# Moving the two halves of the normalised activations to other addresses, 256 and 128 bytes off the weights modulo 512

## The chip, the cores and the metric

The kernel runs on one core of one Trainium2 chip. The metric is the device time of one execution in microseconds, taken as the median of three runs.

## The reference, cut to what matters

A decoder trunk of two layers, 256 tokens wide 1024. Layer 0 mixes tokens with a dilated sliding window (three head groups of eight heads), layer 1 with block-sparse attention, which at 256 tokens is plain causal attention over one block (16 heads). Each layer ends in a squared-ReLU MLP of width 4096.

```python
for i in range(DEPTH):                       # 2
    u = rmsnorm(h, norm_mix[i])
    h = h + (dsw_mixer if i % 2 == 0 else moba_mixer)(u, w_qkv, q_gain, k_gain, w_o, rel_bias)
    h = h + sq_relu_mlp(rmsnorm(h, norm_ffn[i]), ffn_w1[i], ffn_w2[i])

def sq_relu_mlp(h, w1, w2):
    return jnp.square(jax.nn.relu(h @ w1)) @ w2
```

All inputs and outputs are float32.

## The kernel before, in words

Every large product is computed in split precision. A weight slice of 128 rows by 512 columns comes from HBM into a `raw` buffer; ScalarE writes its rounded part `hi` and VectorE the rest `lo` (`next_hi`, line 158, and `next_lo`, line 173). The activations are split in the same way. A product is then three TensorE matmuls: high by high, high by low, low by high. `mm3` (line 230) issues them for the attention projections and for the second MLP product; `up` (line 629) writes them out for the first (lines 654 to 656).

`u` is the transposed activation, before its row norm is applied (the norm's factor is multiplied in later). It stands in four SBUF tiles: `uh` and `ul` (high and low part) of half 0 (rows 0 to 511 of the model width) and of half 1. `norm_transpose` (line 347) makes them: four TensorE transposes of `h` into PSUM, a copy on ScalarE (line 362), a subtraction on VectorE (line 363). Each tile is 128 partitions by 4 chunks of 256 float32, that is 4096 bytes in a partition. `ux(k, cols)` (line 404) gives chunk `k`, from half `k // 4`.

`u` is used in two places, in opposite roles:

- `project` (line 411), the q, k and v projections of both layers (tiles `acc_a`, `acc_b`). The chunk of `u` for one half of the tokens (128 columns, 512 bytes in a partition) is the stationary operand, loaded by LDWEIGHTS; the weight slice of 512 columns is the moving one. For each of 15 groups of columns and each half of the tokens, `k` runs from 0 to 7: twelve matmuls on half 0 of `u`, then twelve on half 1.
- `ffn`'s `up(j)`, `j` from 0 to 7 (tile `up`). Here 128 columns of a weight slice (512 bytes) are stationary and a chunk of `u` (256 columns, 1024 bytes) moves. For `j` of 1 and more, `c` runs over four column blocks and `k` from 0 to 7 inside it, so again twelve matmuls on half 0 and twelve on half 1 take turns. For `j` of 0 all of half 0 comes first.

The other large products, `down(j)` of the MLP (tile `y`) and `wo_group` (tiles `wo_a`, `wo_b`), don't use `u`: a hidden or attention tile (`hh`, `hl`, `oh`, `ol`) is stationary, and a weight slice moves. An MLP runs `up(0)`, `up(1)`, `down(0)`, `up(2)`, `down(1)` and so on to `down(7)`.

The order of work is written out by hand; weight splitting and small work are placed between the matmuls by `beat` and `defer`.

Addresses follow from the order in which pools and tiles are declared, and from their sizes, each rounded up to 32 bytes. The tiles that hold weights (`raw`, `hi`, `lo`), hidden values and attention outputs all start at a multiple of 512 bytes in the partition. Ahead of the four tiles of `u` lie `spread` (1028 bytes, from a multiple of 512) and `warm`, of which one element is used:

```python
    warm = const.tile([P, 33], F32, name="warm")                    # line 275
    ...
        if t == 0:                                                  # line 349
            u[half] = tuple(ut.tile([P, 4, S], F32R, tag=f"u{half}{s}", bufs=1, name=f"u{s}_{which}_{half}")
                            for s in ("h", "l"))
```

1028 bytes take 1056, which is 32 modulo 512; `warm` with 132 bytes takes 160; so all four tiles of `u`, each 4096 bytes long, start 192 bytes past a multiple of 512.

Of the kernel before, what the change touches and what calls it, by code (L numbers as in the profile page):

```python
# [24 lines left out]
F32 = mybir.dt.float32  # L25
F32R = mybir.dt.float32r
# [4 lines left out]
P = 128  # L31
S = 256
# [35 lines left out]
def trunk(ctx, tc, x, rel_bias, norm_mix, norm_ffn, a_w_qkv, a_q_gain, a_k_gain, a_w_o,  # L68
# [6 lines left out]
    const = ctx.enter_context(tc.tile_pool(name="const", bufs=1))  # L75

    ut = ctx.enter_context(tc.tile_pool(name="ut", bufs=1))
# [5 lines left out]
    def bank(tag, name):  # L83
        return ps.tile([P, 512], F32, tag=tag, bufs=2, name=name)
# [151 lines left out]
    h = const.tile([P, NT, D], F32, name="h")  # L236
# [35 lines left out]
                            pattern=[[-1, S + 1]], channel_multiplier=2)  # L272
    mhalf = lead.tile([P, 16], F32, name="mhalf")
    nc.gpsimd.memset(mhalf, -0.5)
    warm = const.tile([P, 33], F32, name="warm")
    nc.scalar.activation(warm[:, 0:1], ident[:, 0:1], AF.Exp)

    gt = lead.tile([P, 36], F32, name="gt")
# [65 lines left out]
    u = {}  # L344
    rstd = {}

    def norm_transpose(which, half, t, natural):

        if t == 0:
            u[half] = tuple(ut.tile([P, 4, S], F32R, tag=f"u{half}{s}", bufs=1, name=f"u{s}_{which}_{half}")  # L350
                            for s in ("h", "l"))
        tp = bank("tp", f"ut_{which}_{half}_{t}")
        for c in range(4):
            k = 4 * half + c
            nc.tensor.transpose(out=tp[:, c * P:(c + 1) * P], in_=h[:, t, k * P:(k + 1) * P], identity=ident)  # L355
        hi, lo = u[half]
        i = tp.rearrange("p (c q) -> p c q", c=4)
        if natural:
            hi, lo = (z.rearrange("p c (q t) -> p t c q", t=NT)[:, t] for z in (hi, lo))
        else:  # L360
            hi, lo = (z[:, :, t * P:(t + 1) * P] for z in (hi, lo))
        nc.scalar.activation(hi, i, AF.Copy)
        nc.vector.tensor_sub(lo, i, hi.bitcast(F32))
# [33 lines left out]
    def norm_half(which, half, natural=False, lead=2):  # L397
        for t in range(NT):
            defer(lead + t, lambda t=t: norm_transpose(which, half, t, natural))
        defer(lead + 3, lambda: norm_squares(which, half))  # L400
        if half == 1:
            defer(lead + 7, lambda: norm_scale(which, natural))
# [287 lines left out]
    for t in range(NT):  # L690
        norm_transpose(0, 0, t, False)
        keep_warm(1)
        for _ in range(2):
            next_hi()
            next_lo()
    for t in range(NT):
        defer(4 + t, lambda t=t: norm_transpose(0, 1, t, False))
# [96 lines left out]
```

## Time and profile before

| | us |
|---|---|
| median of 3 runs | 630.51 (630.36 to 631.11) |
| the profiled execution, device time | 630.4 |
| the profiled execution, span of its instructions | 628.6 |
| TensorE busy | 623.0 (99%) |
| TensorE weight loads busy | 541.2 (86%) |
| VectorE busy | 426.8 (68%) |
| ScalarE busy | 385.1 (61%) |
| DMA engines, mean rate | 181 GB/s |

The span runs from the first to the last instruction; the device time is 1.8 us longer. TensorE's clock was granted in full throughout. Matmuls overlap in their pipeline, so the busy time of TensorE is not a measure of its rate: the rate is read from the distance between the starts of matmuls that follow each other, and the duration that a row gives for one matmul grows with that distance.

### The profile page before, as it was taken

How to read it: one execution, taken by the hardware profiler on the slowest of the kernel's cores; microseconds unless marked ns; L12 is line 12 of the kernel's file. 1: busy time of each engine (PE TensorE's matmuls, PEld its weight loads, DVE VectorE, ACT ScalarE, POOL GpSimd, SP SyncE). 2: the span in 40 equal slices, each digit the busy share in tenths (PEclk: the TensorE clock that was granted, in tenths of full speed). 3: DMA queues.
4: the chain of work that ended last, by engine and by line, in shares of the span. 5: the costliest groups of instructions: out<-in, count | busy, mean ns of one | idle time of the engine just before them, and what ended most of it. 6: DMA issues, size and time to landing. Idle time of an engine off the chain costs nothing.

```text
span 628.6 us, 10380 instructions
## 1 busy us (share of the span) xinstructions
PE 623.0 (99%) x3902; PEld 541.2 (86%) x3902; DVE 426.8 (68%) x767; ACT 385.1 (61%) x742; POOL 36.6 (6%) x23
## 2 busy tenths in 40 slices
PE   8999999999999999999999999999999999999997
PEld 7778887888989989998988878778998899899886
DVE  5877988856875476467547789887776745754651
ACT  6866876765765356456537868777665644663540
POOL 1222221000000000000000332000000000000000
PEclk9999999999999999999999999999999999999999
DMA  7977456433655563574556657563467446645801
GB/s 250 315 196 241 124 187 174 163 108 124 215 174 190 205 223 140 187 254 140 174 179 202 196 180 195 142 186 125 157 211 260 147 161 230 220 127 191 250 18 68
DMA packets 74539, 113.62 MB, mean 181 GB/s; under 512 B 4585, under 2 KB 30505, under 8 KB 74489
## 3 DMA queue, kind: packets, MB, share of 16 engines
q1 hardware_dynamic: 74312, 112.82, 55.7%
q8 instruction: 31, 0.51, 0.3%
q14 instruction: 20, 0.16, 0.1%
q10 hardware_dynamic: 176, 0.14, 0.1%
HBM read 111.81 MB, written 1.13 MB: 180 GB/s over the span
## 4 chain that ended last, share of the span: by engine, by line
PE 97%; DVE 1%; DMA 1%; ACT 0%; issue 0%; DVEq 0%; SPq 0%; ACTq 0%
PE up L654 10%; PE up L656 9%; PE up L655 9%; PE y L231 9%; PE y L233 9%; PE y L232 9%; PE acc_a L231 6%; PE acc_a L232 5%; PE acc_a L233 5%; PE acc_b L231 3%; PE acc_b L233 3%; PE acc_b L232 3%; PE s_a L520 1%; PE o_a L585 1%; PE ut L355 1%; PE wo_b L231 1%
## 5 line engine op out<-in xcount | busy, mean ns | idle before, releaser
L179 DVE SCALAR_TENSOR_TENSOR lo<-raw,gt,hi 128x512 fp32r<-128x512 f32 x248 | 174.6, 745 | 7.4 <-ACT hi L169 7.2
L169 ACT ACTIVATE hi<-raw,gt 128x512 fp32r<-128x512 f32 x248 | 163.0, 714 | 5.7 <-PE y L233 2.8
L654 PE MATMUL up<-uh,hi 128*128 128x256 f32 x512 | 143.6, 281 | 0.0
L655 PE MATMUL up<-ul,hi 128*128 128x256 f32 x512 | 143.3, 280 | 0.0
L656 PE MATMUL up<-uh,lo 128*128 128x256 f32 x512 | 143.3, 280 | 0.0
L177 DVE TENSOR_TENSOR lo<-raw,hi 128x512 fp32r<-128x512 f32 x152 | 98.0, 685 | 42.0 <-ACT hi L167 41.8
L167 ACT ACTIVATE hi<-raw 128x512 fp32r<-128x512 f32 x152 | 88.1, 624 | 52.6 <-PE up L655 20.2
L231 PE MATMUL y<-hi,hh 128*128 128x512 f32 x256 | 99.8, 390 | 0.0
L233 PE MATMUL y<-hi,hl 128*128 128x512 f32 x256 | 99.6, 389 | 0.0
L232 PE MATMUL y<-lo,hh 128*128 128x512 f32 x256 | 99.6, 389 | 0.0
L656 PEld LDWEIGHTS up<-uh,lo 128*128 128x128 f32 x512 | 97.8, 191 | 0.0
L655 PEld LDWEIGHTS up<-ul,hi 128*128 128x128 f32 x512 | 96.1, 188 | 0.6
L654 PEld LDWEIGHTS up<-uh,hi 128*128 128x128 f32 x512 | 96.1, 188 | 0.5
L640 DVE TENSOR_TENSOR r<-r 128x512 f32<-128x512 f32 (+1 forms) x36 | 22.7, 631 | 65.6 <-ACT r L638 65.6
L638 ACT ACTIVATE r<-up 128x512 f32<-128x512 f32 (+1 forms) x36 | 19.8, 550 | 72.8 <-PE up L656 72.4
L231 PE MATMUL acc_a<-hi,uh 128*128 128x512 f32 x144 | 60.6, 421 | 0.0
L232 PE MATMUL acc_a<-lo,uh 128*128 128x512 f32 x144 | 57.0, 396 | 0.0
L233 PE MATMUL acc_a<-hi,ul 128*128 128x512 f32 x144 | 56.9, 395 | 0.0
L233 PEld LDWEIGHTS y<-hi,hl 128*128 128x128 f32 x256 | 48.0, 188 | 10.0
L231 PEld LDWEIGHTS y<-hi,hh 128*128 128x128 f32 x256 | 48.1, 188 | 9.4
L232 PEld LDWEIGHTS y<-lo,hh 128*128 128x128 f32 x256 | 48.1, 188 | 9.4
L231 PE MATMUL acc_b<-hi,uh 128*128 128x512 f32 x96 | 40.1, 418 | 0.0
(128 smaller groups left out, 777.4 us busy)
## 6 DMA issues: line engine op xcount, KB each, us to landing
raw<-in_ffn_w_dram SPq DMA_DIRECT2D x128, 512.0 KB, 4.9
raw<-in_a_w_qkv_dram SPq DMA_DIRECT2D x64, 256.0 KB, 4.3
raw<-in_b_w_qkv_dram SPq DMA_DIRECT2D x24, 512.0 KB, 4.6
raw<-in_b_w_o_dram SPq DMA_DIRECT2D x8, 512.0 KB, 5.0
bias_a<-vdram_a SPq DMA_DIRECT2D x20, 128.0 KB, 6.0
raw<-in_a_w_qkv_dram SPq DMA_DIRECT2D x4, 512.0 KB, 6.6
raw<-in_a_w_o_dram SPq DMA_DIRECT2D x4, 512.0 KB
bias_b<-vdram_b SPq DMA_DIRECT2D x8, 256.0 KB, 4.5
```

Source lines behind the costliest of these rows:

```text
L167: nc.scalar.activation(hi, w, AF.Copy)
L169: nc.scalar.activation(hi, w, AF.Copy, scale=gt[:, gain + c:gain + c + 1])
L177: nc.vector.tensor_sub(lo, w, hi.bitcast(F32))
L179: nc.vector.scalar_tensor_tensor(lo, w, gt[:, gain + c:gain + c + 1], hi.bitcast(F32), op0=ALU.mult, op1=ALU.subtract)
L231: nc.tensor.matmul(acc, lhsT=a[0], rhs=b[0], start=first, stop=False)
L232: nc.tensor.matmul(acc, lhsT=a[0], rhs=b[1], start=False, stop=False)
L233: nc.tensor.matmul(acc, lhsT=a[1], rhs=b[0], start=False, stop=last)
L638: defer(1, lambda: nc.scalar.activation(r, banks[b][:, :w], AF.Relu))
L640: defer(3, lambda: nc.vector.tensor_mul(r, r, r))
L654: nc.tensor.matmul(o, lhsT=whi[:, cols], rhs=uh, start=k == 0, stop=False)
L655: nc.tensor.matmul(o, lhsT=whi[:, cols], rhs=ul, start=False, stop=False)
L656: nc.tensor.matmul(o, lhsT=wlo[:, cols], rhs=uh, start=False, stop=k == 7)
```

## The change

`warm` grows from 33 to 49 elements. It takes 224 bytes in place of 160, so that the first tile of `u` starts at 256 modulo 512. The low part of half 0 gets 96 more float32, 384 bytes that nothing reads or writes, behind its data; so the tiles of half 1 start at 256 + 384, which is 128 modulo 512. The tiles keep their shape for all who use them.

```diff
-    warm = const.tile([P, 33], F32, name="warm")
+    warm = const.tile([P, 49], F32, name="warm")
@@
         if t == 0:
-            u[half] = tuple(ut.tile([P, 4, S], F32R, tag=f"u{half}{s}", bufs=1, name=f"u{s}_{which}_{half}")
-                            for s in ("h", "l"))
+            n = {"h": 4 * S, "l": 4 * S + (96 if half == 0 else 0)}
+            u[half] = tuple(ut.tile([P, n[s]], F32R, tag=f"u{half}{s}", bufs=1, name=f"u{s}_{which}_{half}")
+                            [:, 0:4 * S].rearrange("p (c q) -> p c q", c=4) for s in "hl")
```

No instruction is added, removed or moved.

## Rows read from the trace of the kernel before

**Rows 1.** The page: span, TensorE's busy time, clock, and the chain that ended last
```profile
span 628.6 us, 10380 instructions
PE 623.0 (99%) x3902; PEld 541.2 (86%) x3902; DVE 426.8 (68%) x767; ACT 385.1 (61%) x742; POOL 36.6 (6%) x23
PEclk9999999999999999999999999999999999999999
PE 97%; DVE 1%; DMA 1%; ACT 0%; issue 0%; DVEq 0%; SPq 0%; ACTq 0%
```
**Rows 2.** Waits of TensorE: waiting line, awaited one, us in total, times, longest
```profile
PE warm_ps L261 <- DVE idle L255: 1.1, 1, 1.1
PE ut L355 <- DMA h<-in_x_dram: 0.6, 1, 0.6
```
**Rows 3.** The page's costliest groups: line, shapes, count, busy us, mean ns of one
```profile
L654 PE MATMUL up<-uh,hi 128*128 128x256 f32 x512 | 143.6, 281 | 0.0
L231 PE MATMUL acc_a<-hi,uh 128*128 128x512 f32 x144 | 60.6, 421 | 0.0
L231 PE MATMUL acc_b<-hi,uh 128*128 128x512 f32 x96 | 40.1, 418 | 0.0
```
**Rows 4.** Timeline of TensorE, start and duration in us: `up(0)`, `up(1)`, then `down(0)`
```profile
156.88 0.60 PE L355 MATMUL ut<-ident,h 128*128 128x128 f32 x4
...
157.68 0.28 PE L654 MATMUL up<-uh,hi 128*128 128x256 f32 x1
...
176.03 0.28 PE L654 MATMUL up<-uh,hi 128*128 128x256 f32 x1
...
176.38 0.39 PE L231 MATMUL y<-hi,hh 128*128 128x512 f32 x1
...
177.07 0.39 PE L231 MATMUL y<-hi,hh 128*128 128x512 f32 x1
```
**Rows 5.** Timeline of TensorE: `up(2)` from its first matmul, then `down(1)`, then `up(3)`
```profile
187.27 0.28 PE L654 MATMUL up<-uh,hi 128*128 128x256 f32 x1
...
198.58 0.39 PE L231 MATMUL y<-hi,hh 128*128 128x512 f32 x1
...
209.46 0.28 PE L654 MATMUL up<-uh,hi 128*128 128x256 f32 x1
```
**Rows 6.** Groups of instructions from 158 to 176 us (`up(0)`, `up(1)`)
```profile
L655 PE MATMUL up<-ul,hi 128*128 128x256 f32 x54 | 14.9, 276 | 0.0
L654 PE MATMUL up<-uh,hi 128*128 128x256 f32 x53 | 14.6, 276 | 0.0
```
**Rows 7.** Groups of instructions from 187.3 to 331 us (`up(2)` to `down(7)`, layer 0)
```profile
L655 PE MATMUL up<-ul,hi 128*128 128x256 f32 x192 | 54.0, 281 | 0.0
L232 PE MATMUL y<-lo,hh 128*128 128x512 f32 x110 | 42.8, 389 | 0.0
```
**Rows 8.** Groups of instructions from 479.5 to 615 us (the same in layer 1)
```profile
L654 PE MATMUL up<-uh,hi 128*128 128x256 f32 x192 | 54.0, 281 | 0.0
```
**Rows 9.** Timeline of TensorE: `project` of layer 1, a stretch that nothing else interrupts
```profile
341.10 0.39 PE L232 MATMUL acc_b<-lo,uh 128*128 128x512 f32 x1
...
352.77 0.39 PE L232 MATMUL acc_b<-lo,uh 128*128 128x512 f32 x1
```
**Rows 10.** Timeline of TensorE: output projection of layer 1, such a stretch
```profile
435.71 0.50 PE L231 MATMUL wo_b<-hi,oh_b 128*128 128x512 f32 x1
436.04 0.40 PE L232 MATMUL wo_b<-lo,oh_b 128*128 128x512 f32 x1
436.28 0.39 PE L233 MATMUL wo_b<-hi,ol_b 128*128 128x512 f32 x1
...
437.20 0.39 PE L231 MATMUL wo_b<-hi,oh_b 128*128 128x512 f32 x1
...
442.41 0.39 PE L233 MATMUL wo_b<-hi,ol_b 128*128 128x512 f32 x1
```
**Rows 11.** Instructions on tile `uh`: count, ns min/median/max, first and last start
```profile
L656 PEld LDWEIGHTS up<-uh,lo x512: 187/192/192, 153.8 to 602.6; 128*128 128x128 f32 x171
L362 ACT ACTIVATE uh<-ut x16: 576/598/643, 5.3 to 450.8; 128x512 fp32r<-128x512 f32 x16
L363 DVE TENSOR_TENSOR ul<-ut,uh x16: 680/692/693, 5.9 to 451.5; 128x512 fp32r<-128x512 f32 x16
```

## The prediction, made before the changed kernel was run

> **What bounds the kernel now.** I read the page first. TensorE is busy for 623.0 of 628.6 us at full clock, and 97% of the chain that ended last is its own [rows 1]. The waits of TensorE name two, 1.1 and 0.6 us, both in the first microseconds [rows 2]. No other engine holds it up. So the time can only change with the distance from one matmul to the next, and the question is which matmuls stand further apart than they must.
>
> The page can't tell, since it averages: 281 ns for a matmul of `up`, 418 to 421 for the first of each triple of `acc` [rows 3], the latter with the gaps behind transposes in it. So I went to the timeline and divided the distance of two starts by the matmuls between them.
>
> - `up(0)` and `up(1)`: 157.68 to 176.03 us holds 162 matmuls, 113.3 ns each [rows 4].
> - `up(2)`: 187.27 to 198.58 us holds 96, 117.8 ns each [rows 5]. Same shape, same lines, same addresses modulo 512.
> - `down(1)`, the same stretch further: 198.58 to 209.46 us, 48 matmuls of 512 columns, 226.7 ns each [rows 5], just twice 113.3.
> - `project`, undisturbed: 341.10 to 352.77 us, 51 matmuls, 228.8 ns [rows 9].
> - `wo_b`, undisturbed: 437.20 to 442.41 us, 23 matmuls, 226.5 ns [rows 10].
>
> The groups of instructions by stretch confirm that these are not chosen spots: a matmul of `up` lasts 276 ns from 158 to 176 us [rows 6] and 281 ns in all of `up(2)` to `up(7)`, in both layers [rows 7, 8]. Twelve of the sixteen `up` stages therefore run at the wide pace (117.8 ns) and four at the narrow one (113.3).
>
> Two things are to be seen here. First, with stationary and moving operand both at 0 modulo 512 (`y`, `wo`) the matmuls settle at 226.7 ns; with the stationary one at 192 (`acc`) they stay 2.1 ns above it for as long as the stretch lasts. So the offset plausibly matters. Second, `up` shows both 113.3 and 117.8 ns at one and the same offset. So the offset alone doesn't decide; how a stage is entered does, and it then persists: 162 matmuls narrow, 96 wide, none in between. The wide pace follows a `down`, the narrow one follows transposes. The excess is regular, 13.3 ns in three matmuls of `up` (3 x 4.45) and about 6.5 in three of `acc` (3 x 2.15), one about twice the other, which looks like a step of some 6.7 ns lost once or twice in three matmuls (an estimate of mine, worked out from these distances).
>
> **The change part by part.** It moves no instruction. What it changes is three relations.
>
> *`up`, wide stages.* 12 stages x 96 = 1152 matmuls x (117.8 - 113.3) = 5.1 us [rows 4, 5, 7, 8]. This is the most that `up` can give. The moving `u` goes from 192 off the weights to 256 in the first twelve matmuls of each column block, and to 128 in the second twelve. No row shows either offset. The bounds of what they cost per matmul: from below, 0 over the narrow pace; from above, the nearest thing is a pace with three steps in three matmuls in place of two, that is 6.7 ns over the narrow one, 2.2 more than now. Over 1152 matmuls that is -5.1 to +2.6 us.
>
> *`up`, narrow stages.* 4 stages x 96 = 384 matmuls. They have nothing to win. If they fall to the wide pace they lose 384 x 4.45 = 1.7 us.
>
> *`acc`.* 15 groups x 2 x 8 x 3 = 720 matmuls, at most 720 x 2.15 = 1.5 us to win against the 226.7 of `y` [rows 5, 9]. To lose: as much again, if one step in three becomes two, 1.5 us.
>
> *The border between the halves.* New is that within one stage the relation jumps every twelve matmuls. Before, both halves lay alike and nothing jumped. No row shows such a jump; the nearest are two changes of operands. Where a narrow `up` meets `down(0)`, three matmuls from 176.38 to 177.07 us take 0.69 us against 0.68 when settled, 10 ns lost [rows 4]. Behind other work, `wo_b` needs 240 ns for one matmul and 230 each for four (436.28 to 437.20) where 226.5 is settled, 27 ns lost [rows 10]. I take 10 ns, since operands follow each other there without a pause, as at the border. There are 7 jumps in each of 14 `up` stages and 1 in each of 2, 100 in all, and in `project` 4 for each group but a layer's first, 54 in all: 154 jumps, 0 to 1.5 us at 10 ns, 4.2 us at 27. Below nothing it can go as well, because a jump that meets the wide pace can end it; that is counted with the stages.
>
> *What else moves.* The slack behind `ul` of half 0 is neither written nor read. The writers of `u` are 16 copies of 598 ns and 16 subtractions of 692 ns in the whole program [rows 11]; were each 10% slower, it would be 32 x 0.065 = 2.1 us of work on engines that are busy 61 and 68% of the span, and TensorE waits for neither in any row [rows 1, 2]. Without that cover it would be the 2.1 us. The small tiles behind `u` shift too; they hold a few numbers per partition. I put all this at nothing.
>
> *Which value I take.* For `up` in its wide stages, one of the two halves at the narrow pace and the other as now: 576 x 4.45 = 2.6 us won. The reason is the persistence: the wide pace lasts because each of 96 matmuls finds the same relation, the narrow pace lasts for the same reason, and of the two offsets now met in turn I take it that one is entered so that the narrow pace is reached. Each return into it costs a jump, 10 ns, four times in each of 12 stages: 0.5 us lost. For `acc` and the narrow stages, no change. Sum: 2.6 - 0.5 = 2.1 us won against the profiled execution's 630.4 us (628.6 of span and 1.8 around it, which stays), so 628.3; the median of the runs shown stands 0.1 above that execution, so 628.4.
>
> *A rule against this.* In `acc` and `y` the same moving operand (a weight slice at 0) stands further apart when the loaded one lies at 192: 228.8 against 226.7 ns [rows 5, 9]. The Trainium skill, TensorE: Matmul & The Clock Gate, section "Step-by-step: what each phase is for", says that TensorE has two independent read ports on SBUF and that loading the next weights takes no read bandwidth from the running matmul. By that rule no offset matters and the change is worth 0; the rows of `acc` and `y` speak against it, though not finally, since the two stages also differ in what runs beside them.
>
> **The rivals.**
>
> *No change: the pace is set by history, not by address.* For it: `up` shows both rates at one offset [rows 4, 5], so a stage might keep its rate wherever `u` lies; and 256 and 128 lie evenly on both sides of 192, so what one half wins the other may lose. Against it: `acc` never reaches the 226.7 ns that `y` and `wo` reach within some matmuls [rows 9, 10]. Result 630.5, from 629.3 to 631.7. That the change doesn't do what it says, because the tiles land elsewhere, ends here too; the sizes and the rounding to 32 bytes leave little room for it.
>
> *Slower: the jumps break the narrow stages.* The narrow pace needs an undisturbed run; a jump every twelve matmuls throws `up(0)` and `up(1)` of both layers to the wide pace (1.7 us), and each jump costs some matmuls of settling (0 to 1.5 us, at the far bound 4.2), while the wide stages stay as they are, because both offsets hold the same conflict. Result 630.5 + 1.7 + 0 to 1.5 = 632.2 to 633.7, at the far bound 636.4. It decides from the point where the first matmuls behind a jump stand over 113.3 ns apart in `up(0)`, whose single jump is easy to find. For it: 10 ns were lost where operands change at the narrow pace [rows 4]. Against it: `up(0)` is cut by transposes at 156.88 us and is at the narrow pace again from 157.68 at the latest [rows 4], so a disturbance need not end in the wide one.
>
> *Much faster: all of `up` narrow, and `acc` at the rate of `y`.* 5.1 + 1.5 = 6.6 us: 623.9. For it: nothing but that both rates exist. Against it: it needs both offsets, in both roles, to be free of loss.
>
> **How the numbers follow.** A measurement of this kernel can tell about 0.2%, 1.3 us, from no change. Forecast, part of the loss in `up` is gone: 0.32, from 626.0 to 629.2, most likely 628.4. Much faster: 0.10, 623.9 to 626. No change: 0.28. Slower: 0.30, of which the ends beyond 633 hold a third. The range leaves out the far end of "much faster" and the far end of "slower", about 0.1 each: 625.0 to 633.0. The forecast's own range is 626.0 to 629.2, since cases of both signs hold much. Faster by over 0.2%: 0.42; within: 0.28; slower: 0.30.
>
> **What would show it.** Right: in a wide stage such as the one that began at 187.27 us, the distance alternates every twelve matmuls between about 113.3 and 117.8 ns, and the durations of `up` by stretch show 276 beside 281; `y` and `wo` stay at 389 ns; `acc` stays near 228.8. The stage's 96 matmuls then take about 11.1 us in place of 11.31. Also to be read: LDWEIGHTS of the low weights, 192 ns at the median now against 187 at the least [rows 11], which should fall in the narrow half. Wrong: `up` at 117.8 throughout (no change), `up(0)` and `up(1)` at 281 ns (slower), or a change in `y`, which doesn't use `u` at all and would mean that the reason is another. A share of VectorE's or ScalarE's waits in the chain would mean that something I put at nothing isn't.

## The result, and the profile after

The changed kernel is slower: 635.64 us in the median of 4 runs (634.71 to 635.72) against 630.78 us (630.36 to 631.11, 4 runs) of the kernel before on the same chip, a ratio of 1.0076 with a 95% interval from 1.0064 to 1.0088. The profiled execution took 635.72 us, of which 633.9 us are span; the 1.8 us around it stayed. So 5.3 us more of span are to be found in this pair of profiles.

The page of the changed kernel answers [rows 1]: span, TensorE, its clock by slices, the chain that ended last.

```profile
span 633.9 us, 10380 instructions
PE 627.2 (99%) x3902; PEld 544.5 (86%) x3902; DVE 427.4 (67%) x767; ACT 385.8 (61%) x742; POOL 36.6 (6%) x23
PEclk8999999999999999999999999999999999999999
PE 96%; DVE 1%; DMA 1%; ACT 1%; issue 0%; SPq 0%; DVEq 0%; ACTq 0%
```

Nothing has taken the bound away from TensorE: still 99% busy, still nearly the whole chain. One digit differs, the first of the clock. The rest must again be in the distance from matmul to matmul.

Groups of instructions, first of 158 to 176 us (`up(0)`, `up(1)`; lines are one higher than before), to be held against [rows 6]:

```profile
L656 PE MATMUL up<-ul,hi 128*128 128x256 f32 x50 | 14.1, 282 | 0.0
```

and of 187.3 to 331 us (`up(2)` to `down(7)` of layer 0), to be held against [rows 7]:

```profile
L655 PE MATMUL up<-uh,hi 128*128 128x256 f32 x192 | 54.1, 282 | 0.0
...
L232 PE MATMUL y<-lo,hh 128*128 128x512 f32 x111 | 43.2, 390 | 0.0
```

`up` was at 276 and 281 ns; now it is at 282 ns in both kinds of stage. The narrow stages are gone, and the wide ones have become a little wider. The timeline of TensorE gives the pace (start, duration; the stretches of [rows 4] and [rows 5]):

```profile
159.05 0.28 PE L656 MATMUL up<-ul,hi 128*128 128x256 f32 x1
...
177.98 0.28 PE L656 MATMUL up<-ul,hi 128*128 128x256 f32 x1
...
189.48 0.28 PE L655 MATMUL up<-uh,hi 128*128 128x256 f32 x1
...
190.92 0.28 PE L655 MATMUL up<-uh,hi 128*128 128x256 f32 x1
...
192.34 0.28 PE L655 MATMUL up<-uh,hi 128*128 128x256 f32 x1
...
200.90 0.40 PE L231 MATMUL y<-hi,hh 128*128 128x512 f32 x1
...
211.82 0.28 PE L655 MATMUL up<-uh,hi 128*128 128x256 f32 x1
```

- `up(0)` and `up(1)`: 159 matmuls from 159.05 to 177.98 us, 119.1 ns each, where it was 113.3.
- `up(2)`: 96 matmuls from 189.48 to 200.90 us, 119.0 ns each, where it was 117.8. Its first twelve, on half 0, take 1.44 us, the twelve on half 1 behind them 1.42 us. Two decimals are too few for a pace over twelve: by the starts in ns these are 119.3 and 119.0 ns each, and over the 14 stages with seven jumps both halves average 119.0. Neither half is anywhere near 113.3.
- `down(1)`: 48 matmuls from 200.90 to 211.82 us, 227.5 ns, where it was 226.7.

`project` of layer 1, the stretch of [rows 9], twelve matmuls on half 0 of `u` and then twelve on half 1:

```profile
348.15 0.39 PE L231 MATMUL acc_b<-hi,uh 128*128 128x512 f32 x1
...
350.88 0.40 PE L231 MATMUL acc_b<-hi,uh 128*128 128x512 f32 x1
...
353.68 0.40 PE L231 MATMUL acc_b<-hi,uh 128*128 128x512 f32 x1
```

Half 0 takes 227.5 ns for each, half 1 about 233; before, both stood at 228.8.

Adding up all distances from one start to the next by stage, in both traces, gives the account (us, sums of my own from the starts):

| stage | before | after | difference | of which |
|---|---|---|---|---|
| `up` | 179.71 | 183.08 | +3.37 | four stages that were narrow, 2.0 together; twelve that were wide, about 1152 x 1.2 ns = 1.4 |
| `acc_a`, `acc_b` | 174.82 | 176.20 | +1.38 | half 1, about 360 x 2.2 ns = 0.8; half 0, nothing behind the start; the rest, 0.6, is the first 13 us |
| `y` | 174.11 | 174.56 | +0.45 | the first six matmuls of each `down` |
| all else | | | +0.1 | |

That is the 5.3 us. Two entries need a word. In `y` each of the 14 `down`s that follow an `up` now begins with distances of 235, 231, 236, 228, 233 and 231 ns before it settles at 226.7, since it is entered out of `up` in another step than before: 34 ns, 14 times.

The other is the start. Timeline of the changed kernel:

```profile
9.20 0.63 PE L233 MATMUL acc_a<-hi,ul 128*128 128x512 f32 x1
9.63 0.63 PE L231 MATMUL acc_a<-hi,uh 128*128 128x512 f32 x1
...
12.13 0.39 PE L231 MATMUL acc_a<-hi,uh 128*128 128x512 f32 x1
```

and of the kernel before:

```profile
9.08 0.63 PE L233 MATMUL acc_a<-hi,ul 128*128 128x512 f32 x1
9.51 0.63 PE L231 MATMUL acc_a<-hi,uh 128*128 128x512 f32 x1
...
10.64 0.40 PE L231 MATMUL acc_a<-hi,uh 128*128 128x512 f32 x1
```

In both, matmuls of 512 columns stand 0.43 us apart at first and 0.23 us later; the change comes at about 10.4 us before and at about 12.1 us in the changed kernel. A stretch of one microsecond in the changed kernel (columns: stretch and its length, TensorE's busy time and instructions, granted clock as a fraction of the 2.4 GHz level, DMA share, GB/s) shows it at 1.2 GHz:

```profile
11.00:12.00 1.00, 1.00 (x4) 0.50 1.08 381
```

The page of the kernel before shows full clock from the first slice on [rows 1], and so the text in front of the prediction says "throughout". But its trace holds no record of the clock ahead of 10.43 us, and the page counts time without a record as full; its matmuls stood 0.43 us apart there, just as those of the changed kernel did at a recorded 0.50.

The waits of TensorE in the changed kernel, against [rows 2]:

```profile
PE ut L356 <- DMA h<-in_x_dram: 0.9, 1, 0.9
PE acc_a L231 <- ACT hi L169: 0.5, 1, 0.5
PE acc_a L232 <- DVE lo L179: 0.3, 1, 0.3
```

They come to 1.1 us more than before, but that isn't time lost: behind them the third matmul of `acc_a` starts only 0.12 us later than before (9.20 and 9.08 us). They stand ahead of the fall of the clock, which in this trace was granted in full from 5.2 us and at half from 8.6 to 12.05 us. In all, the first transposes of the second half of `u` come at 12.83 us in place of 12.03. This 0.8 us is no work of the change: run e9 below, whose stages all keep the old pace, starts later still (13.23 us), e5, with other offsets again, earlier (11.85 us), and 13 runs of the kernel before on one chip lie between 630.20 and 632.13 us. So of the 5.3 us about 4.5 are the change's.

### The profile page after: what moved, and what is told of

It is laid out like the page before. It is cut to its first block, busy times and chain, and to the rows that moved or that the text cites. A ratio compares the mean times of both kernels' runs of the same rounds, so it can differ in the third digit from the quotient of the medians.

```text
span 633.9 us, 10380 instructions
## 1 busy us (share of the span) xinstructions
PE 627.2 (99%) x3902; PEld 544.5 (86%) x3902; DVE 427.4 (67%) x767; ACT 385.8 (61%) x742; POOL 36.6 (6%) x23
## 4 chain that ended last, share of the span: by engine, by line
PE 96%; DVE 1%; DMA 1%; ACT 1%; issue 0%; SPq 0%; DVEq 0%; ACTq 0%
PE up L655 10%; PE up L657 10%; PE up L656 10%; PE y L233 9%; PE y L232 9%; PE y L231 9%; PE acc_a L231 6%; PE acc_a L232 5%; PE acc_a L233 5%; PE acc_b L231 3%; PE acc_b L233 3%; PE acc_b L232 3%; PE s_a L521 1%; PE o_a L586 1%; PE wo_b L231 1%; PE pt_a L564 1%
```

## The experiments

At the start these theories stood against each other. A: each offset of `u` has a settled pace of its own in each of its two roles, and the jumps between the halves matter little. A1: the offset has one price for both roles, so that what is good in `acc` is good in `up`. B: the offsets are harmless, the jumps every twelve matmuls do the damage. C: at one offset two paces can hold, and the way in chooses. D: other work beside TensorE makes the difference, or the size and place of other tiles.

### One half's offset for both, and the halves exchanged

e1 has both halves at 256, e2 both at 128; neither has a jump.

```diff
-    warm = const.tile([P, 33], F32, name="warm")
+    warm = const.tile([P, 49], F32, name="warm")      # e1: 49, e2: 17; u as in the kernel before
```

> All four tiles of u at 256 modulo 512, no jump between the halves. Theory A (each offset has its own settled pace, the jumps cost little): matmuls of up settle at 120.0 ns, as they do at the end of each twelve on half 0 in the changed kernel, in all sixteen stages, that is 2.2 x 1152 + 6.7 x 384 ns = 5.1 us more than before; acc settles at 226.7 ns, as it does there on half 0, up to 1.2 us less; 634 to 635 us. Theory B (the loss comes from the jumps between the halves, either offset alone is no worse than 192): up at 117.8 ns or less after each down and 113.3 ns in the first two stages, 630.5 us or less.

> All four tiles of u at 128 modulo 512, no jump. Theory A: up settles near 118.8 ns, the mean of the repeating five distances 120, 119, 115, 118, 122 that half 1 shows in the changed kernel, in all stages: 1.0 x 1152 + 5.5 x 384 ns = 3.3 us more than before; acc near 231 to 232 ns, some 1.5 us more; about 635 us. Theory B: 630.5 us or less, as for 256.

e1: 634.93 us (634.72 to 635.58), ratio 1.007, 1.0055 to 1.0085. e2: 638.43 us (636.63 to 638.48), ratio 1.0115, 1.0095 to 1.0135. `up(2)` with the first matmul behind it, and 36 matmuls of `project` of layer 1, in the timeline of e1:

```profile
188.76 0.28 PE L655 MATMUL up<-uh,hi 128*128 128x256 f32 x1
...
200.27 0.40 PE L231 MATMUL y<-hi,hh 128*128 128x512 f32 x1
...
347.84 0.39 PE L231 MATMUL acc_b<-hi,uh 128*128 128x512 f32 x1
...
356.00 0.39 PE L231 MATMUL acc_b<-hi,uh 128*128 128x512 f32 x1
```

and of e2:

```profile
190.65 0.28 PE L655 MATMUL up<-uh,hi 128*128 128x256 f32 x1
...
202.17 0.39 PE L231 MATMUL y<-hi,hh 128*128 128x512 f32 x1
...
350.04 0.40 PE L231 MATMUL acc_b<-hi,uh 128*128 128x512 f32 x1
...
358.41 0.40 PE L231 MATMUL acc_b<-hi,uh 128*128 128x512 f32 x1
```

In e1 `up` stands at 119.9 ns (11.51 us over 96) and `acc` at 226.7 (8.16 us over 36); in e2 at 120.0 and 232.5. So without a single jump the loss is all there: B falls. The offset that is best for `acc`, 256, is the worst for `up`: A1 falls as well. The jumps even help a little: with them `up` takes 183.08 us, without them 184.51 (256) or 184.12 (128). On half 0 the first eight or so matmuls behind a jump are not yet settled at 120.0; on half 1 the distances repeat 120, 119, 115, 118 and 122 ns, a mean of 118.7, which is the pace of e2's `up(0)` and `up(1)` and not the 120.0 of its other stages.

e3 puts half 0 at 128 and half 1 at 256, by 17 elements of `warm` and 32 float32 of slack.

```diff
-    warm = const.tile([P, 49], F32, name="warm")
+    warm = const.tile([P, 17], F32, name="warm")
@@
-            n = {"h": 4 * S, "l": 4 * S + (96 if half == 0 else 0)}
+            n = {"h": 4 * S, "l": 4 * S + (32 if half == 0 else 0)}
```

> The halves of the changed kernel exchanged: half 0 at 128, half 1 at 256 modulo 512. Theory A: the same two paces change places (up 120.0 ns at the end of each twelve on half 1, the five distances on half 0; acc 226.7 ns on half 1), total within 1 us of the changed kernel, 634.6 to 636.6 us. Theory B: the same number of jumps and so the same loss, 635.6 us; but if a single direction of the jump does the harm, another time.

634.95 us (634.66 to 636.71), ratio 1.0075, 1.0057 to 1.0092. The paces go with the offset, not with the half: now the last matmuls on half 1 stand at 120.0 ns in `up` and settle at 226.7 in `acc`, and half 0 shows 232.5 in `acc`.

### Same offsets, other places

e4 leaves both halves at 192 modulo 512, but moves half 1 by 512 bytes, with the same kind of slack that the change brought in. e9 moves half 1 by 256 bytes, to 448.

```diff
-    warm = const.tile([P, 49], F32, name="warm")
+    warm = const.tile([P, 33], F32, name="warm")
@@
-            n = {"h": 4 * S, "l": 4 * S + (96 if half == 0 else 0)}
+            n = {"h": 4 * S, "l": 4 * S + (128 if half == 0 else 0)}      # e4: 128, e9: 64
```

> Half 0 at 192 as before, half 1 also at 192 modulo 512 but 512 bytes further up than before, so that the tiles are cut and spaced as in the changed kernel without a change modulo 512. Theories A and B alike: nothing changes, 630.5 us, up 113.3 ns in the first two stages and 117.8 ns after each down, acc 228.9 ns. A theory by which the spacing of the tiles, the padded tile or the shift of the small tiles does the harm: 632 to 636 us.

> Half 0 at 192, half 1 at 448 modulo 512, so that the relation jumps by 256 at each border of the halves. If the pattern repeats every 256 bytes, as the kernels at 0 and 256, 64 and 320, 128 and 384 suggest: nothing changes against before, 113.3 ns in the first two stages of up, 117.8 ns after each down, acc 228.9 ns, 630.2 us. If it repeats every 512, another pace on half 1 and other totals.

e4: 630.23 us (630.07 to 632.10, 10 runs), ratio 0.9995, 0.9984 to 1.0006. `up(2)` of e4:

```profile
187.02 0.28 PE L655 MATMUL up<-uh,hi 128*128 128x256 f32 x1
...
198.32 0.39 PE L231 MATMUL y<-hi,hh 128*128 128x512 f32 x1
```

11.30 us over 96 matmuls, before 11.31, and every stage's sum is that of before within 0.05 us, apart from the first 13 us. So slack, moved tiles and shifted small tiles cost nothing, and that half of D falls; the other half, work beside TensorE, falls with e11 and e14 below. e9: 631.7 us in one run beside 630.59; `up`, `y` and `acc_b` take 179.71, 174.11 and 69.40 us, as before to the hundredth, and the 1.2 us more lie in the first 13 us. An offset of 448 is thus the same as one of 192.

### A row of offsets

One run each, both halves alike, by the size of `warm`: 113 elements for 0, 1 for 64, 65 for 320, 81 for 384, 41 for 224.

```diff
-    warm = const.tile([P, 33], F32, name="warm")
+    warm = const.tile([P, 113], F32, name="warm")     # e5: 113, e6: 1, e7: 65, e8: 81, e10: 41
```

> All four tiles of u at 0 modulo 512, as the weights. Theory A1 (what counts is the offset of the loaded operand from the moving one, in any stage): acc has then the offset of y and must settle at 226.7 ns as y does; up has the offset 0 too and should settle at 113.3 ns everywhere: 630.8 less 5.1 and up to 1.6 us, about 624 us. Theory A2 (each role has its own dependence on the offset, since in up weight loads follow each other without a pause): acc 226.7 ns all the same, up anywhere between 113.3 and 120.0 ns, 624 to 634 us.

> All four tiles at 64 modulo 512. A1 and A2: acc between 226.7 (0, 256) and 233 ns (128); up between 113.3 and 120 ns; a point of the curve, 624 to 639 us. If the offsets are of no matter for up after a down, 117.8 ns.

> All four tiles at 320 modulo 512: u then stands to the weights in up as the weights stood to u in acc at 192. A1: up settles at the pace that acc has at 192, one lost step in three matmuls, 115.6 ns, and acc at the one that up has at 192 after a down, two lost steps in three, 231.1 ns: 630.8 - 2.5 + 1.0 + 1.6 = about 631 us. A2: no such exchange.

> All four tiles at 384 modulo 512, the mirror of 128. A1: up as acc at 128, that is 2.5 to 3 lost steps in three matmuls, about 119 to 120 ns; acc as up at 128, 231 to 233 ns: 636 to 639 us. A2: no such exchange.

> All four tiles at 224 modulo 512, between 192 (up 113.3 or 117.8, acc 228.9 ns) and 256 (up 120.0, acc 226.7 ns). If only the 64-byte block counts, as 192: 630.2 us. If the place inside the block counts as well, paces between or outside those, 627 to 636 us.

Paces in ns, once settled, by stage, and the sums of `up` and `acc_b` in us, from the starts of each trace (`acc_b` rather than `acc_a`, since the start of the span lies in `acc_a`):

| offset of both halves | run | time, us | `up(0)`, `up(1)` | `up(2)` to `up(7)` | `acc` | sum of `up` | sum of `acc_b` |
|---|---|---|---|---|---|---|---|
| 0 | e5 | 634.77 | 120.0 | 120.0 | 226.7 | 184.50 | 69.14 |
| 256 | e1 | 634.93 | 120.0 | 120.0 | 226.7 | 184.51 | 69.14 |
| 64 | e6 | 635.32 | 117.8 | 117.8 | 233.3 | 181.28 | 70.37 |
| 320 | e7 | 635.53 | 117.8 | 117.8 | 233.3 | 181.28 | 70.37 |
| 128 | e2 | 638.43 | 118.7 | 120.0 | 232.5 | 184.12 | 70.07 |
| 384 | e8 | 636.56 | 118.6 | 120.0 | 232.5 | 184.12 | 70.06 |
| 192 | before | 630.78 | 113.3 | 117.8 | 228.9 | 179.71 | 69.40 |
| 224 | e10 | 636.37 | 118.3 | 118.3 | 233.3 | 182.08 | 70.15 |

In both sums, pairs that differ by 256 bytes agree to 0.01 us (their times differ by up to 1.9 us, most of it in the start of `acc_a`). A1 had 624 us for e5 and 631 for e7, and missed both. What counts is the offset modulo 256, not modulo 512 as the change's own words have it; its two offsets are 0 and 128 in that measure. The weights lay at 0 modulo 512 in every run, so whether the place of `u` counts by itself or its distance from the weights is not separated. Inside the 256 bytes nothing tried comes near 192, and 224 shows that 32 bytes off it are enough to lose. Two of the traces, e6 (`up(2)` at 117.8 ns, `acc` at 233.3):

```profile
189.85 0.28 PE L655 MATMUL up<-uh,hi 128*128 128x256 f32 x1
...
201.16 0.40 PE L231 MATMUL y<-hi,hh 128*128 128x512 f32 x1
...
348.00 0.40 PE L231 MATMUL acc_b<-hi,uh 128*128 128x512 f32 x1
...
356.40 0.40 PE L231 MATMUL acc_b<-hi,uh 128*128 128x512 f32 x1
```

and e10 (`up(2)` at 118.3 ns):

```profile
190.48 0.28 PE L655 MATMUL up<-uh,hi 128*128 128x256 f32 x1
...
201.84 0.40 PE L231 MATMUL y<-hi,hh 128*128 128x512 f32 x1
```

At 64 the wide pace stands in all sixteen `up` stages, `up(0)` and `up(1)` too. The narrow pace occurs at 192 (and 448, e9) alone. So A holds as far as the offset and the role decide which paces there are, but not as one pace for each: 192 has 113.3 and 117.8, and 128 and 384 have two as well, 118.6 to 118.7 and 120.0, again by what comes ahead of the stage. What is left is C.

### The way in

The kernel before has a case of C that the prediction passed over. In layer 1 `up(0)` is entered straight from `wo_b`; its first 18 matmuls, up to the transposes that cut it, stand at the wide pace, and behind the transposes the same stage, at the same addresses, settles at the narrow one (timeline of before; 17 distances in 2.00 us, then 21 in 2.38):

```profile
446.95 0.28 PE L654 MATMUL up<-uh,hi 128*128 128x256 f32 x1
...
448.95 0.28 PE L656 MATMUL up<-uh,lo 128*128 128x256 f32 x1
...
451.36 0.28 PE L654 MATMUL up<-uh,hi 128*128 128x256 f32 x1
...
453.74 0.28 PE L654 MATMUL up<-uh,hi 128*128 128x256 f32 x1
```

e11 and e12 leave `u` at 192 and send one more matmul ahead of the first of each `up(j)` from `j` = 2 on, over 258 or 268 columns; the first matmul proper starts its bank anew and so overwrites it. e14 is the same with 256 columns, a shift by no more than a whole matmul.

```diff
                     cols = slice(c * P, (c + 1) * P)
+                    if j >= 2 and c == 0 and k == 0:
+                        nc.tensor.matmul(banks[b][:, 0:258], lhsT=whi[:, cols],      # e12: 268, e14: 256
+                                         rhs=u[0][0].rearrange("p c q -> p (c q)")[:, 0:258], start=True, stop=True)
                     nc.tensor.matmul(o, lhsT=whi[:, cols], rhs=uh, start=k == 0, stop=False)
```

> The kernel before with one matmul more at the head of each up after a down (12 in all): the first one is issued twice, the first time over 258 columns in place of 256, its result overwritten; so the 96 that follow start some 0.8 ns later than they would behind 256. Theory C (at 192 both paces are stable, and the entry picks one): if the shift reaches the narrow pace, 96 matmuls at 113.3 ns in those stages, 12 x (96 x 4.45 - 133) ns = 3.5 us less, 626.7 us; if it falls short of it, 117.8 ns as before and 12 x 118 ns = 1.4 us more, 631.6 us. Theory D (it is what runs beside that sets the pace): 631.6 us.

> As the run with 258 columns, but 268: the entry is shifted by 5 ns. Theory C: one of the two shifts, or both, lead to the narrow pace: 626.7 us, else 631.6 us. Theory D: 631.6 us.

> The control of the run at 258: one more matmul at the head of each up(j) from j = 2 on, but with 256 columns, so the entry is not shifted by a width of its own. Entry theory: the stage meets the same pattern one matmul later and stays at 117.8 ns; 12 matmuls more, 12 x 0.118 = 1.4 us, so 632.0 us. Rival, that any additional matmul at the head lets the stage settle at 113.3 ns: 626.8 us.

e11: 626.85 us in one run beside 630.59; e12: 628.70; e14: 632.88 beside 631.25. e12 has neither of the times expected for it, though `up` takes 176.34 us in both e11 and e12: 1.7 us of the 1.85 between them lie in `acc_a`, that is in the start. `up(2)`, now of 97 matmuls, in e11:

```profile
186.88 0.28 PE L655 MATMUL up<-uh,hi 128*128 128x258 f32 x1
...
197.90 0.39 PE L231 MATMUL y<-hi,hh 128*128 128x512 f32 x1
```

and in e14:

```profile
187.94 0.28 PE L655 MATMUL up<-uh,hi 128*128 128x256 f32 x1
...
199.37 0.40 PE L231 MATMUL y<-hi,hh 128*128 128x512 f32 x1
```

11.02 us for 97 matmuls is 113.6 ns, 11.43 us is 117.8. In e11 the first distances are 118, 124, 119, 118, 118, 114 and from there on 113.3 in all twelve stages; in e12 they are 123, 119, 120, 118, 119 and then 113.3 as well. In e14 the wide pace is there from the first to the last. The additional matmul does nothing by itself; the two columns do it. C is shown for 192: both paces keep themselves up there, and the first matmul of the stage chooses between them. That it does so by shifting the entry a few ns is the likely reading, but not shown by itself: 2 and 12 columns more both lead to the narrow pace, and nothing between or beyond was tried. A widened first matmul wasn't tried at any other offset.

e13 drops the additional matmul and widens the first of the stage instead; the two surplus columns belong to the next column block, whose own start overwrites them.

```diff
-                    nc.tensor.matmul(o, lhsT=whi[:, cols], rhs=uh, start=k == 0, stop=False)
+                    if j >= 2 and c == 0 and k == 0:
+                        nc.tensor.matmul(banks[b][:, 0:258], lhsT=whi[:, cols],
+                                         rhs=u[0][0].rearrange("p c q -> p (c q)")[:, 0:258], start=True, stop=False)
+                    else:
+                        nc.tensor.matmul(o, lhsT=whi[:, cols], rhs=uh, start=k == 0, stop=False)
```

> No matmul is added. The first matmul of each up(j) from j = 2 on, 12 in all, takes 258 columns in place of 256; the two surplus columns of its result are overwritten by the later start of the next column block. Entry theory (at 192 both paces hold, a shift of the entry by a few ns chooses): 113.3 ns after some six matmuls in all 12 stages, and since the extra matmuls of the run at 258 (12 x 0.118 = 1.4 us) are gone, 626.85 - 1.4 = 625.4 us. Rival, that the additional matmul and not its width mattered: 117.8 ns throughout, 630.6 us.

626.70 us (625.68 to 627.60, 5 runs) beside 631.25 (630.02 to 632.11, 11 runs): ratio 0.9929, 0.9915 to 0.9943, faster than both kernels. Timeline of `up(2)`, and the group of `up` from 187.3 to 331 us, that before showed 281 ns:

```profile
188.02 0.28 PE L655 MATMUL up<-uh,hi 128*128 128x258 f32 x1
...
198.93 0.39 PE L231 MATMUL y<-hi,hh 128*128 128x512 f32 x1
```

```profile
L659 PE MATMUL up<-ul,hi 128*128 128x256 f32 x192 | 53.1, 277 | 0.0
```

96 matmuls in 10.91 us; `up` as a whole takes 174.98 us, 4.73 less than before, and each `down` loses 0.015 us on its way in. The median is 1.3 us over the expected 625.4; the profiled execution starts as late as that of the changed kernel did, with the transposes of the second half at 12.77 us where e11, from which the 625.4 was worked out, has them at 11.63. So 1.1 us of the excess are the late start.

e15 adds an offset for each role: `u` of the attention's norms, which `project` reads, 64 bytes further, at 256; `u` of the MLP's, which `up` reads, at 192. The size of the joint tile puts half 1 at 512 and 448, which is the same modulo 256.

```diff
-            u[half] = tuple(ut.tile([P, 4, S], F32R, tag=f"u{half}{s}", bufs=1, name=f"u{s}_{which}_{half}")
-                            for s in ("h", "l"))
+            f = 0 if which % 2 else 16
+            hl = ut.tile([P, 8 * S + 64], F32R, tag=f"u{half}", bufs=1, name=f"u_{which}_{half}")
+            u[half] = tuple(hl[:, f + 4 * S * m:f + 4 * S * (m + 1)].rearrange("p (c q) -> p c q", c=4) for m in range(2))
```

> The widened first matmul, and u at another offset in each role: 256 in the mixers' norms (project), 192 in the MLP's (up). Offset by role: acc falls to the 226.7 ns at which it ran with both halves at 256 or 0, where its stages together took 0.6 us less than at 192 (174.4 to 173.9 us); up stays at 113.3 ns. So 625.4 - 0.6 = 624.8 us. Rival, that the gain of acc is lost again on the way in, or that h and l sharing a tile adds a wait: 625.4 us or more.

625.13 us (624.95 to 626.73, 6 runs), ratio 0.9914, 0.9899 to 0.9929. Timeline, `up(2)` and 36 matmuls of `project` of layer 1:

```profile
186.61 0.28 PE L656 MATMUL up<-u,hi 128*128 128x258 f32 x1
...
197.52 0.39 PE L231 MATMUL y<-hi,hh 128*128 128x512 f32 x1
...
342.04 0.39 PE L231 MATMUL acc_b<-hi,u 128*128 128x512 f32 x1
...
350.20 0.39 PE L231 MATMUL acc_b<-hi,u 128*128 128x512 f32 x1
```

Both are at their best, 113.6 and 226.7 ns. By the sums of `acc`, 173.89 us against 174.49 in e11, whose `u` is at 192 and which starts as early, the second offset is worth 0.6 us; the times of e13 and e15 overlap and can't show so little by themselves.

## Why the prediction was wrong, point by point

*What bounds the kernel* was right but for the first 10.4 us, whose matmuls stood as far apart as those of the changed kernel at a recorded 0.50: the whole difference lies in the distances of matmuls, with the share of TensorE unchanged, and VectorE and ScalarE where they were (DVE 1% of the chain before and after).

*`up`, wide stages: the step that failed.* I took it that of the two offsets met in turn one would be entered so that the narrow pace is reached, and booked 2.6 us for it. No row showed either offset, and neither shows a narrow pace in any of the kernel's own ways into a stage: alone, 256 stands at 120.0 ns in every `up` stage, 128 at 118.7 to 120.0. The upper bound of that term, three steps in three matmuls and 2.2 ns above the wide pace, is just what 256 does. Taken over 1152 matmuls it gave 2.6 us of loss; at the 119.0 ns that both halves average in turn, it came to 1.4. So this term, 2.6 us won in the sum, was 1.4 us lost.

The error has a root further up. From two paces at one offset I concluded that the narrow pace is something that a good entry can reach at other offsets too. With the entries that were tried it is found at 192 alone; whether another entry reaches it elsewhere is open. The kernel before stood at the best place for `up`, and what it lacked was the entry.

*`up`, narrow stages.* Booked as no change, with 1.7 us as the loss if they fell to the wide pace. They fell further, to 119.0 ns, 2.0 us. It is the largest single term of the result, and the forecast had it at nothing. e6 shows the 1.7 as such: at 64 these four stages run at 117.8 and the sum of `up` grows by 1.57 us.

*`acc`.* Booked as no change, 1.5 us either way. Half 0 settles at 226.7, but takes as long in sum as before, since the first matmuls behind each jump give the gain back; half 1 went to 233: about 0.8 us of loss, inside the bound. The reading that the offset matters there, from `acc` at 228.8 beside `y` at 226.7, was right, and e1 and e6 show it within one stage: 226.7 at 256, 233.3 at 64. The rule of the Trainium skill that I weighed there (TensorE: Matmul & The Clock Gate, "Step-by-step: what each phase is for"), two independent read ports and no bandwidth taken from the running matmul by the loading of weights, doesn't speak of offsets; I read from it that every offset costs the same. Between e1 and e6 nothing but the offset differs, and the pace does by 6.7 ns, so what the rule leaves out decides here.

*The jumps.* 0.5 us counted as loss, up to 4.2 at the far bound. They cost nothing in `up`; against either offset alone they gave back 1.0 to 1.4 us.

*What else moves* at nothing: right, by e4 and e9.

*Not foreseen: `y`.* I wrote that a change in `y` would mean that the reason is another. It was the same one: `y` settles at 226.7 ns as ever, but each `down` needs six matmuls to get there, 0.45 us in all.

*The rivals.* "Slower: the jumps break the narrow stages" had the direction and part of the place, with 632.2 to 633.7 us; that 635.64 lies below its far bound of 636.4 is luck, since that bound pays 4.2 us for jumps, which cost nothing in `up`. Its test, a first matmul behind a jump over 113.3 ns apart in `up(0)`, doesn't apply: `up(0)` stands at 120 ns ahead of its single jump already. Its mechanism is refuted by e1 and e2, which have no jump and are no faster. Nor did it hold that the wide stages stay as they are. "No change: history, not address" fell with e4 beside e1. "Much faster" needed both offsets free of loss; its time, 623.9, is nearly reached by e15, at other offsets.

*The signs that I named.* The alternation of 113.3 and 117.8 ns isn't there; both halves average 119.0. The stage of 96 matmuls took 11.42 us, not 11.1. And the weight loads mislead. Instructions on tile `uh` in the changed kernel, against [rows 11]:

```profile
L657 PEld LDWEIGHTS up<-uh,lo x512: 187/189/192, 155.0 to 607.9; 128*128 128x128 f32 x171
```

The median fell from 192 to 189 ns while the matmuls moved apart; here the duration of a load didn't follow the pace.

## What to carry to other kernels

Two paces at one address are a question about the entry, so try the entry (a first matmul two columns wider) before moving the tile: here that was worth 0.7%, and the move cost 0.8%. An address is judged in each role that the tile has, moving and stationary, by the settled distance of starts in each; what suits one role can be the worst for the other, and then two offsets for one tile's two uses are to be had for a few hundred bytes. Where the price of an offset stands in no row of the trace, the stages that are now at their best belong into the sum as losses, not as "no change".

## What the runs showed of the hardware that I had not expected

- The pace of these float32 matmuls hangs on the place of `u` modulo 256 bytes in the partition, in eight offsets tried, with the weights always at 0: 113.3 to 120.0 ns with 256 columns and `u` moving, 226.7 to 233.3 ns with 512 columns and `u` stationary, and not in the same order.
- Three settled distances are multiples of one step of 6.67 ns: 113.3 is 17 steps, 120.0 (at 0 and 256) is 18, 226.7 is 34. The others fit averages of whole steps over three to eight matmuls; 117.8 is 53 steps in three (arithmetic of mine from the starts; with so many matmuls to choose from, a fit says little). That the two paces at 192 keep themselves up, and that two columns at the entry choose, fits a matmul that must begin in step with something; what that is no run here shows.
- The rate of the first matmuls differs from run to run: those of 512 columns stand 0.43 us apart at first, and come to 0.23 us at about 10.4 us in the profile of before, 12.1 us in that of the changed kernel and 12.9 us in e9. It moves the start of the second half's transposes by up to 1.8 us (11.63 us in e11, 13.46 in e12), more than the smaller effects here; the stage sums of `up`, `y` and `acc_b` are free of it. The granted clock goes with it wherever a trace has a record of it: in the changed kernel 0.50 up to 12.05 us, in e9 full from 12.86 us on. The view shows 1.00 for e9 from 6 to 12 us only because there is no record. Why the clock rises at another time in each run wasn't tried.
